# Weight loads in 1 MB pieces at set points, first loads in one queue, and decay ahead of v, q, k

## Chip, cores, metric

One Trainium2 chip, all 8 cores. Each core runs the same program on one prompt sequence and 16 of the 128 sample sequences. The metric is the device time in microseconds (us) of the slowest core. A program on 8 cores has executions in a slower state, in which the cores of one die show a lower granted clock; only fast executions are compared here. In the profiles PE is TensorE (PEld its weight loads), DVE is VectorE, ACT is ScalarE, POOL is GpSimd and SP is SyncE.

## The reference, cut

Two layers of a decoder trunk, for 2,064 prompt tokens per sequence (16 learned meta tokens ahead) and 4 new tokens of every sample sequence:

```python
xn = rmsnorm(h, norm_g)
q, k, v, ga, u, gb, alow, mg = split(xn @ w_in)          # 6160 columns
la = log_sigmoid(alow @ w_alpha + b_alpha) / 16          # data-dependent decay, per key channel
# branch A: gated linear attention with decay exp(cumsum(la)), recurrent state S (128 x 256 per head)
# branch B: trailing means over 2/4/8/16 positions minus the token, a small linear map
ya = (norm(o) * gain * silu(ga)) @ w_a
yb = (pool * scale * silu(gb)) @ w_b
h = h + (sig(mg_A) * ya + sig(mg_B) * yb) @ w_out
```

Outputs are the final normed activations and the new attention and pooling states.

## The kernel before

Each layer has two phases. Phase 1 walks over the prompt in 8 pairs of 128-token tiles (p = 0 to 7) and a last tile of 80 tokens (16 prompt, 64 sample): projections, decay, attention, pooling. Phase 2 walks over the pairs again: `merge` (output gates, `w_a`, `w_b`; 8 column blocks c a pair) and `out_tile` (`w_out`), with the work on the 16 sample states spread between the merges.

The weights of the two phases do not fit together. They share two SBUF regions, V (v, q, k; later six of the merge blocks) and RR (gates, u; later the last two merge blocks and `w_out`). So four times 17 to 19 MB of f32 weights are read and cast to bf16 on the way, which the kernel does on the POOL queue. All other transfers go through the SP queue.

Every operation goes into a list. A small scheduler with modelled durations then fixes the order on each engine ahead of time: lowest list index first among those ready by its model. Each engine executes its order strictly in order, and semaphores are derived from overlaps of memory. So an engine that waits for one thing holds up what is listed behind it.

```python
def load_w1_v(l, after):                 # v, q, k of layer l: 5 pieces
    for a, b in ((0, O_Q), (O_Q, O_K), (O_K, O_V), (O_V, O_V + 4096), (O_V + 4096, N_V1)):
        dma(V1[:, a:b], w1[l, :, a:b], eng="pool", after=after)
def load_w1_r(l): ...                    # gates, u: 4 pieces of 2 MB, into RR
def load_w2_v(l, after): ...             # merge blocks 0..5: 6 pieces, into V
def load_w2_r(l): ...                    # merge blocks 6, 7 and w_out: 4 pieces, into RR

def front(l, p):                         # normed, transposed input of pair p
    if l == 0:
        for i, t in enumerate(tiles_of(p)):
            h = hb[t % 2][0:n, :]        # two tile buffers
            if t >= 2:
                dma(h, hin[r0:r0 + n, :])
            norm_t(0, h, n, t, xn_of(p)[:, :, i * 128:i * 128 + n])   # ACT, POOL, DVE, 8 PE transposes, DVE
        ...
    elif p < NPAIR:
        dma(xnT[p % 2], XN[1][p], ...)   # layer 1: loaded, phase 2 of layer 0 made it

def phase1(l):
    front(l, 0); front(l, 1); decay(l, 0); decay(l, 1)
    for f_ in (q_proj, k_proj):
        f_(0); f_(1)
    for t in range(4):
        v_proj(t // 2, t % 2)
    for p in range(NPAIR):
        if p >= 2:
            q_proj(p); k_proj(p); v_proj(p, 0)
        if p >= 1:
            decay(l, p + 1)
        if p >= 2:
            v_proj(p, 1)
        k_tok(p, k_)                     # 8 PE transposes of k
        scores(p, 0, q_, k_); gate_a(l, p, 0)
        bo0 = attend(p, 0, q_, v_of(2 * p))
        scores(p, 1, q_, k_); gate_a(l, p, 1)
        normalise(bo0, 128, on[0], 0)
        bo1 = attend(p, 1, q_, v_of(2 * p + 1))
        pool_u(l, p)
        normalise(bo1, 128, on[1], 1)
        gate_b(l, p)
        gate_o(on[0], ...)
        if p + 2 <= NPAIR:
            front(l, p + 2)
        pool_y(l, p)
        gate_o(on[1], ...)
        ...
        if p == 2:
            load_w2_v(l, [len(S.ops) - 1])
    # ... last tile, load_w2_r(l), new states out

def phase2(l):
    sample_load(l, 0); sample_load(l, 1)
    for j in range(NPAIR + 1):           # pairs; c = column blocks
        for c in range(8):
            merge(l, j, c)
            if j > 0 and c in (1, 3):
                out_tile(l, j - 1, c // 2)
            # sample work: state s is loaded, cast on ACT, multiplied, updated, stored
        if j == 2 and l + 1 < NL:
            load_w1_v(l + 1, [len(S.ops) - 1])
    ...
```

(Cuts are marked by dots.)

Of the kernel before, what the change touches and what calls it, by code (L numbers as in the profile page):

```python
# [14 lines left out]
NL = 2  # L15
# [14 lines left out]

O_AL, O_Q, O_K, O_V = 0, 128, 128 + 4096, 128 + 8192
N_V1 = 128 + 8192 + 8192
# [18 lines left out]
class Sched:  # L51
# [69 lines left out]
    def list_schedule(self):  # L121
# [15 lines left out]
        for i in range(n):  # L137
            if npred[i] == 0:
                heapq.heappush(pend[ops[i]["eng"]], (0.0, i))
        order = []  # L140
        while len(order) < n:
            best = None
            for e in engs:
                T = free_t[e]
                while pend[e] and pend[e][0][0] <= T:
                    heapq.heappush(avail[e], heapq.heappop(pend[e])[1])
                if avail[e]:
                    st_, idx = T, avail[e][0]
                elif pend[e]:
                    st_, idx = pend[e][0]  # L150
                else:
                    continue
                if best is None or (st_, idx) < (best[0], best[1]):
                    best = (st_, idx, e)
            st_, idx, e = best
            if avail[e] and avail[e][0] == idx:
                heapq.heappop(avail[e])
            else:
                heapq.heappop(pend[e])
            op = ops[idx]  # L160
            if op["dma"]:
                issue = 60.0 if e == "sp" else 900.0
                free_t[e] = st_ + issue
                dma_free[e] = max(st_ + issue, dma_free[e]) + op["cost"]
                done_t[idx] = dma_free[e] + 1800.0
            else:
                free_t[e] = st_ + op["cost"]
                done_t[idx] = st_ + op["cost"] + op["lat"]
            order.append(idx)
            for j, soft in succ[idx]:  # L170
                rt_ = free_t[e] if soft else done_t[idx]
                if ready_t[j] < rt_:
                    ready_t[j] = rt_
                npred[j] -= 1
                if npred[j] == 0:
                    heapq.heappush(pend[ops[j]["eng"]], (ready_t[j], j))
        self.sim_end = max(done_t)
        if __import__("os").environ.get("SIMEND"): print("sim_end", self.sim_end)
        remap = {old: new for new, old in enumerate(order)}
# [176 lines left out]
def build_nc():  # L356
# [34 lines left out]
    with contextlib.ExitStack() as st:  # L391
# [178 lines left out]
        def dma(out, in_, r=(), w=(), eng="sp", after=(), **kw):  # L570
            nb = 1
            for d_ in list(out.shape):
# [4 lines left out]
            return S.add(eng, lambda e: e.dma_start(out=out, in_=in_, **kw), r=list(r) + sb_r, w=list(w) + sb_w,  # L577
                         dma=True, after=after, cost=nb / 220.0)

# [9 lines left out]

        cft = f32(base, NCF)  # L590
        h_first = [dma(hb[t], hin[128 * t:128 * (t + 1), :]) for t in range(2)]
        dma(cft, cf_d[:, :])
        dma(cols, cols_d[:, :])
        cp("dve", ident_f, cft[:, CF_ID:CF_ID + 128])
        cp("dve", ident_b, cft[:, CF_ID:CF_ID + 128])
# [12 lines left out]

        def load_w1_v(l, after):
            for a, b in ((0, O_Q), (O_Q, O_K), (O_K, O_V), (O_V, O_V + 4096), (O_V + 4096, N_V1)):  # L610
                dma(V1[:, a:b], w1[l, :, a:b], eng="pool", after=after)

        def load_w1_r(l):
            for a, b in ((0, 4096), (4096, 8192), (8192, 12288), (12288, N_R1)):
                dma(RR[:, a:b], w1[l, :, N_V1 + a:N_V1 + b], eng="pool")

        def load_w2_v(l, after):
            for c in range(N_EARLY_C):
                dma(V2[:, c * CB:(c + 1) * CB], w2[l, :, c * CB:(c + 1) * CB], eng="pool", after=after)

        def load_w2_r(l):
            o = N_EARLY_C * CB
            a = 0
            for b in (CB, 2 * CB, 2 * CB + 4096, N_R2):
                dma(RR[:, a:b], w2[l, :, o + a:o + b], eng="pool")
                a = b

# [37 lines left out]
        def front(l, p):  # L665

            if l == 0:
                for i, t in enumerate(tiles_of(p)):
                    r0, n = rows(t)
                    h = hb[t % 2][0:n, :]  # L670
                    if t >= 2:
                        dma(h, hin[r0:r0 + n, :])
                    norm_t(0, h, n, t, xn_of(p)[:, :, i * 128:i * 128 + n])
# [8 lines left out]

        WQ, WK, WV = V1[:, O_Q:O_K], V1[:, O_K:O_V], V1[:, O_V:N_V1]
        WGA, WU, WGB, WPW = RR[:, 0:O_U], RR[:, O_U:O_GB], RR[:, O_GB:O_PW], RR[:, O_PW:O_PW + 512]
# [294 lines left out]
        def phase1(l):  # L979
            memset("dve", alow[0:17, :], 1.0)  # L980
            dma(walpha[0:17, :], walpha_d[l])
            front(l, 0)
            front(l, 1)
            decay(l, 0)
            decay(l, 1)
            for f_ in (q_proj, k_proj):
                f_(0)
                f_(1)
            for t in range(4):
                v_proj(t // 2, t % 2)  # L990
            for p in range(NPAIR):
                q_, k_ = qk_of(p)
                if p >= 2:
                    q_proj(p)
                    k_proj(p)
                    v_proj(p, 0)
                if p >= 1:
                    decay(l, p + 1)
                if p >= 2:
                    v_proj(p, 1)  # L1000
                k_tok(p, k_)
                scores(p, 0, q_, k_)
                gate_a(l, p, 0)
                bo0 = attend(p, 0, q_, v_of(2 * p))
                scores(p, 1, q_, k_)
                gate_a(l, p, 1)
                normalise(bo0, 128, on[0], 0)
                bo1 = attend(p, 1, q_, v_of(2 * p + 1))
                pool_u(l, p)
                normalise(bo1, 128, on[1], 1)  # L1010
                gate_b(l, p)
                gate_o(on[0], 128, V(eg, 8, 256)[:, :, 0:128], V(oTg[0], 8, 256)[:, :, 0:128])
# [4 lines left out]
                if p < NPAIR - 1:  # L1017
                    dma(OT[p], oTg[0], w=[("OT", p)])
                if p == 2:
                    load_w2_v(l, [len(S.ops) - 1])  # L1020

# [10 lines left out]
            v_proj(p, 0)  # L1032
            load_w2_r(l)
            k_tok(p, k_)
# [132 lines left out]
        def phase2(l):  # L1167
            if l == NL - 1:
                dma(fg, fg_d[:, :])
            for k in range(3):  # L1170
                load_h(l, k)
            sample_load(l, 0)
            sample_load(l, 1)
            bT = banks.one()
# [6 lines left out]
            done = 0  # L1181
            total = 7 * 8 + 2
            for j in range(NPAIR + 1):
                if j + 1 < NPAIR:
                    p2_loads(l, j + 1)
                for c in range(8):
                    merge(l, j, c)
                    if j > 0 and c in (1, 3):
                        out_tile(l, j - 1, c // 2)
                    k = j * 8 + c + 1  # L1190
                    while done < len(units) and done * total < k * len(units):
# [6 lines left out]
                if j == 2 and l + 1 < NL:  # L1198
                    load_w1_v(l + 1, [len(S.ops) - 1])
            out_tile(l, NPAIR, 0)  # L1200
            if l + 1 < NL:
                load_w1_r(l + 1)

        P2_ORDER = [NPAIR - 1] + list(range(NPAIR - 1)) + [NPAIR]
        P2_TILES = [t for p in P2_ORDER for t in tiles_of(p)]
        load_w1_v(0, [h_first[0]])
        load_w1_r(0)
        for l in range(NL):
# [62 lines left out]
```

## Time and profile before

| | before |
|---|---|
| time, median of 3 | 1431.89 us (1428.2 to 1583.76, the last slow) |
| span of the profiled core | 1427.6 us |
| PE (TensorE matmul) busy | 1226.5 us, 86% |
| k transposes of pair 0, layer 0, start at | 115.75 us |
| PE idle at the two phase boundaries | 21.0 and 17.9 us |
| one pair of phase 1, layer 0 / layer 1 | 41.6 / 40.4 us |

The page gives busy tenths in 40 equal slices of 35.7 us. The first two slices of PE are nearly empty, while DMA is at 90% and more:

```profile
span 1427.6 us, 28242 instructions; the slowest of 8 cores (1415.4 to 1427.6 us)
...
PE   0188889998898599699999988999889859999997
...
DMA  9910115710006654975427210641110765455321
```

The chain of work that ended last, in order of time (start, duration, what), says what the start waits for: a table of 36 KB, then two input tiles, which took 29 and 16 us where the median of such a tile is 4.4 us:

```profile
2.44 21.71 DMA arena<-cols
25.99 29.20 DMA arena<-hin
58.63 16.11 DMA arena<-hin
```

The timeline (start, duration, engine, line, operation, and in brackets the idle time before it and what ended that) shows the other holes in PE. At the first boundary SP can issue the sample-state loads (`sgla`) only at 475.40, ACT casts the first at 480.00, and PE had been idle for 20.98 us. The hole at 598.18 is in phase 2 of layer 0, where five weight loads were issued together at 570.37 just ahead of a sample-state load. The hole at 1156.46 is the second boundary.

```profile
475.40 1.56 SPq L577 DMA_DIRECT2D arena<-sgla  x3
480.00 1.06 ACT L532 ACTIVATE arena<-arena 128x1024 bf16<-128x1024 f32 x1 [21.44 <-DMA arena<-sgla]
481.11 19.21 PE L505 MATMUL psum<-arena 128*128 128x4 bf16 x164 [20.98 <-ACT arena L532]
...
570.37 2.77 POOL L577 DMA_DIRECT2D arena<-w  x5 [1.81 <-DMA nsg_s<-arena]
...
598.18 1.03 PE L511 MATMUL psum<-arena 128*128 128x128 bf16 x8 [11.86 <-DVE arena L552]
...
1156.46 8.77 PE L505 MATMUL psum<-arena 128*128 128x4 bf16 x66 [17.86 <-ACT arena L532]
```

In the table of stretches (stretch, length, busy us of PE, PEld, DVE, ACT and POOL with counts, then granted PE clock, DMA share, GB/s), the first two lines cover the boundaries, the others one steady pair of each layer:

```profile
435.00:500.00 65.00, 42.62 (x389) 34.43 (x389) 17.24 (x41) 16.04 (x31) 17.73 (x35) 0.82 0.75 185
1110.00:1180.00 70.00, 50.13 (x453) 40.06 (x455) 20.81 (x47) 18.83 (x36) 20.70 (x41) 0.85 0.71 185
...
280.50:322.10 41.60, 37.86 (x317) 28.79 (x317) 24.10 (x35) 20.91 (x39) 17.37 (x31) 1.00 0.11 41
...
999.20:1039.60 40.40, 36.79 (x302) 27.92 (x301) 20.58 (x31) 18.83 (x35) 15.91 (x27) 1.00 0.10 33
```

So PE idles for 22 us in the 65 of the first boundary and 20 in the 70 of the second, and for 3.6 to 3.7 us in a pair.

### The profile page before, as it was taken

How to read it: one execution, taken by the hardware profiler on the slowest of the kernel's cores; microseconds unless marked ns; L12 is line 12 of the kernel's file. 1: busy time of each engine (PE TensorE's matmuls, PEld its weight loads, DVE VectorE, ACT ScalarE, POOL GpSimd, SP SyncE). 2: the span in 40 equal slices, each digit the busy share in tenths (PEclk: the TensorE clock that was granted, in tenths of full speed). 3: DMA queues.
4: the chain of work that ended last, by engine and by line, in shares of the span. 5: the costliest groups of instructions: out<-in, count | busy, mean ns of one | idle time of the engine just before them, and what ended most of it. 6: DMA issues, size and time to landing. Idle time of an engine off the chain costs nothing.

```text
span 1427.6 us, 28242 instructions; the slowest of 8 cores (1415.4 to 1427.6 us)
## 1 busy us (share of the span) xinstructions
PE 1226.5 (86%) x10552; PEld 949.4 (67%) x10600; DVE 625.7 (44%) x942; ACT 525.7 (37%) x1020; POOL 476.7 (33%) x812
## 2 busy tenths in 40 slices
PE   0188889998898599699999988999889859999997
PEld 0056667667676477588877666676777648778875
DVE  1133555556454244344435255445554324444433
ACT  1025445444542233133334354444445223323332
POOL 2004534344445132222222253434444513232222
PEclk9979799999999699899999999999999979999999
DMA  9910115710006654975427210641110765455321
GB/s 169 197 49 16 52 68 125 164 48 30 23 24 128 209 186 170 178 246 182 171 84 137 54 47 29 125 106 38 38 38 1 143 209 186 170 176 179 142 89 64
DMA packets 41894, 160.28 MB, mean 112 GB/s; under 512 B 5196, under 2 KB 5324, under 8 KB 39164
## 3 DMA queue, kind: packets, MB, share of 16 engines
q1 hardware_dynamic: 36284, 122.49, 24.8%
q0 software_dynamic: 5472, 35.98, 15.6%
q8 instruction: 83, 1.36, 0.4%
q14 instruction: 55, 0.45, 0.1%
HBM read 139.98 MB, written 55.18 MB: 137 GB/s over the span
## 4 chain that ended last, share of the span: by engine, by line
PE 71%; DMA 11%; DVE 8%; issue 4%; ACT 4%; POOL 2%; SPq 1%; DVEq 0%; POOLq 0%; ACTq 0%
PE psum L505 70%; DVE arena L557 6%; DMA nsp_s<-arena 4%; ACT arena L532 3%; DMA arena<-hin 3%; DMA arena<-sgla 2%; DMA arena<-cols 2%; DVE arena L545 1%; PE psum L511 1%; POOL arena L545 1%; POOL arena L552 1%; SPq L577 0%; POOL arena L577 0%; DVE arena L552 0%; DVEq L252 0%
## 5 line engine op out<-in xcount | busy, mean ns | idle before, releaser
L505 PE MATMUL psum<-arena 128*128 128x256 bf16 (+6 forms) x9840 | 1187.2, 281 | 110.0 <-ACT arena L532 61.4
L505 PEld LDWEIGHTS psum<-arena 128*128 128x128 bf16 (+3 forms) x9888 | 904.7, 101 | 376.5 <-ACT arena L532 81.8
L557 DVE SCALAR_TENSOR_TENSOR arena<-arena,psum 128x256 f32<-128x256 f32 (+4 forms) x454 | 262.6, 608 | 370.6 <-PE psum L505 225.3
L545 POOL TENSOR_TENSOR arena<-arena 128x256 bf16<-128x256 f32 (+13 forms) x321 | 275.4, 861 | 266.7 <-DVE arena L557 223.9
L552 POOL TENSOR_SCALAR arena<-arena 128x256 bf16<-128x256 f32 (+5 forms) x389 | 168.0, 441 | 578.3 <-PE psum L505 259.5
L532 ACT ACTIVATE arena<-psum 128x256 bf16<-128x256 f32 (+9 forms) x308 | 198.5, 658 | 336.6 <-PE psum L505 318.9
L532 ACT ACTIVATE arena<-psum,arena 128x256 f32<-128x256 f32 (+2 forms) x356 | 146.9, 456 | 268.6 <-PE psum L505 215.1
L532 ACT ACTIVATE arena<-arena 128x1024 bf16<-128x1024 f32 (+2 forms) x137 | 138.6, 1027 | 261.8 <-DVE arena L557 125.1
L545 DVE TENSOR_TENSOR arena<-psum,arena 128x1024 bf16<-128x1024 bf16 (+4 forms) x120 | 124.6, 1039 | 182.9 <-PE psum L505 129.1
L557 DVE SCALAR_TENSOR_TENSOR arena<-psum,arena 128x256 bf16<-128x256 f32 (+4 forms) x124 | 90.6, 763 | 80.2 <-PE psum L505 79.4
L511 PE MATMUL psum<-arena 128*128 128x128 bf16 (+3 forms) x712 | 55.0, 226 | 81.5 <-DVE arena L552 67.6
L511 PEld LDWEIGHTS psum<-arena 128*128 128x128 bf16 (+3 forms) x712 | 46.7, 101 | 91.6 <-DVE arena L552 68.8
L557 DVE SCALAR_TENSOR_TENSOR arena<-arena 128x256 bf16<-128x256 f32 (+4 forms) x97 | 67.1, 709 | 7.5 <-POOL arena L545 7.2
L552 DVE TENSOR_SCALAR arena<-arena 128x1024 bf16<-128x1024 f32 (+4 forms) x45 | 29.2, 669 | 62.0 <-POOL arena L545 46.5
L552 DVE TENSOR_SCALAR arena<-psum,arena 128x256 bf16<-128x256 f32 (+1 forms) x68 | 29.7, 478 | 59.7 <-POOL arena L545 48.6
L532 ACT ACT_TABLE_LOAD x32 | 41.1, 1283 | 28.2 <-PE psum L505 21.6
L707 DVE TENSOR_TENSOR_SCAN arena<-arena 128x1024 f32<-128x1024 bf16 (+1 forms) x18 | 38.2, 2121 | 8.1 <-ACT arena L532 8.1
L564 POOL COPY arena<-arena 128x4 f32<-128x4 f32 (+4 forms) x56 | 13.6, 242 | 78.3 <-ACT arena L532 59.4
L577 POOL DMA_DIRECT2D arena<-w x38 | 21.4, 578 | 20.3 <-DMA OT<-arena 10.1
L532 ACT ACTIVATION_READ_ACCUMULATOR arena<-psum 128x1 f32 (+1 forms) x136 | 27.0, 199 | 0.0
L532 ACT ACTIVATION_READ_ACCUMULATOR arena<-arena 128x1 f32 (+1 forms) x51 | 9.6, 188 | 0.0
L564 DVE COPY arena<-arena 128x128 f32<-128x128 f32 (+2 forms) x3 | 0.5, 195 | 12.7 <-DMA arena<-cf 12.7
(8 smaller groups left out, 6.3 us busy)
## 6 DMA issues: line engine op xcount, KB each, us to landing
arena<-w POOLq DMA_DIRECT2D x18, 1024.0 KB, 27.0
arena<-hin SPq DMA_DIRECT2D x32, 512.0 KB, 4.4
arena<-sgla SPq DMA_DIRECT2D x32, 512.0 KB, 5.7
nsg_s<-arena SPq DMA_DIRECT2D x32, 512.0 KB, 3.2
arena<-w POOLq DMA_DIRECT2D x16, 896.0 KB, 19.9
arena<-XN SPq DMA_DIRECT2D x22, 512.0 KB, 4.5
H<-arena SPq DMA_DIRECT2D x16, 512.0 KB, 2.8
arena<-H SPq DMA_DIRECT2D x16, 512.0 KB, 4.2
```

Of the source, the lines that this page charges most:

```text
L505: return S.add("pe", lambda e: e.matmul(out, lhsT=lhsT, rhs=rhs, start=start, stop=stop, skip_group_check=sgc), r=[lhsT, rhs], w=[out], co ...
L511: return S.add("pe", lambda e: e.transpose(out, in_, ident), r=[in_, ident], w=[out], cost=c, lat=250.0, attach=True)
L532: return S.add("act", lambda e: e.activation(out=out, in_=in_, func=func, **kw), r=r, w=w, cost=c)
L545: return S.add(eng, lambda e: e.tensor_tensor(out=out, in0=in0, in1=in1, op=op), r=[in0, in1], w=[out], cost=c)
L552: return S.add(eng, lambda e: e.tensor_scalar(out=out, in0=in0, **kw), r=r, w=[out], cost=ecost(eng, fsz(out), 0.55, [out] + r))
L557: return S.add("dve", lambda e: e.scalar_tensor_tensor(out=out, in0=in0, scalar=scalar, in1=in1, op0=op0, op1=op1), r=r, w=[out], cost=eco ...
L564: return S.add(eng, lambda e: e.tensor_copy(out=out, in_=in_), r=[in_], w=[out], cost=ecost(eng, fsz(out), 0.55, (out, in_)))
L577: return S.add(eng, lambda e: e.dma_start(out=out, in_=in_, **kw), r=list(r) + sb_r, w=list(w) + sb_w, dma=True, after=after, cost=nb / 220.0)
L707: S.add("dve", lambda e: e.tensor_tensor_scan(out=B, data0=rm[:, 0:4 * n], data1=A, initial=0.0, op0=ALU.mult, op1=ALU.add), r=[rm[:, 0:4 ...
```

## The change

Its intent: let no weight burst crowd out the small transfers on which PE waits; read the first weights in the order in which they are needed; and in each pair put the long decay chain (matmul, exponentials, scan) under the v matmuls.

1. Weights move in pieces of about 1 MB. Except at the start, `pace()` issues one piece at a set point of the compute, after the operation listed just before it (and two pieces without that wait at each phase boundary).
2. First layer: one queue, in the order alpha, v, q, k, gates, u. Input tiles 2 and 3 go into that queue too. The constants lead the other queue.
3. The pair loop has a new order, and the start runs v ahead of q and k.
4. Sample work in phase 2 starts one pair of merges later.

The core of the diff (cut; the rest moves the column offsets of v, q, k on both sides, and the scheduler's modelled DMA rate):

```diff
-        h_first = [dma(hb[t], hin[128 * t:128 * (t + 1), :]) for t in range(2)]
         dma(cft, cf_d[:, :])
         dma(cols, cols_d[:, :])
+        for t in range(2):
+            dma(hb[t], hin[128 * t:128 * (t + 1), :])
...
+        W1V = [(0, O_V)] + [(O_V + 2048 * i, O_V + 2048 * (i + 1)) for i in range(8)]
+        W1R = ...; W2V = ...; W2R = ...      # pieces of 1792 to 2560 columns
+        def pace(n_=1, after=True):
+            for _ in range(n_):
+                if queue:
+                    d_, s_ = queue.pop(0)
+                    dma(d_, s_, eng="pool", after=[len(S.ops) - 1] if after else ())
...
-                        dma(h, hin[r0:r0 + n, :])
+                        dma(h, hin[r0:r0 + n, :], eng="pool" if t < 4 else "sp")
...
             front(l, 0)
             front(l, 1)
+            if l == 0:
+                pace(len(queue), False)
...
                 if p >= 2:
+                    decay(l, p)
+                    v_proj(p, 0)
+                    v_proj(p, 1)
                     q_proj(p)
                     k_proj(p)
-                    v_proj(p, 0)
-                if p >= 1:
-                    decay(l, p + 1)
-                if p >= 2:
-                    v_proj(p, 1)
                 k_tok(p, k_)
+                gate_a(l, p, 0)
                 scores(p, 0, q_, k_)
-                gate_a(l, p, 0)
-                bo0 = attend(p, 0, q_, v_of(2 * p))
                 scores(p, 1, q_, k_)
                 gate_a(l, p, 1)
+                bo0 = attend(p, 0, q_, v_of(2 * p))
+                pool_u(l, p)
                 normalise(bo0, 128, on[0], 0)
                 bo1 = attend(p, 1, q_, v_of(2 * p + 1))
-                pool_u(l, p)
+                if p == 2:
+                    plan(V2, w2[l], 0, W2V)
+                pace()
+                gate_b(l, p)
                 normalise(bo1, 128, on[1], 1)
-                gate_b(l, p)
...
-            load_w2_r(l)
+            plan(RR, w2[l], N_V2, W2R)
+            pace(2, False)
...
-            total = 7 * 8 + 2
+            total = 6 * 8 + 2
...
+                    if c % 2 == 0 or j == 0:
+                        pace()
-                    k = j * 8 + c + 1
+                    k = j * 8 + c + 1 - 8
+                    if k == -1:
+                        sample_load(l, 0)
+                        sample_load(l, 1)
...
-                    load_w1_v(l + 1, [len(S.ops) - 1])
+                    plan(V1, w1[l + 1], 0, W1V)
```

More of the change, by code (lines that the diff above doesn't have):

```diff
@@ L28 @@
 WINDOWS = (2, 4, 8, 16)
-O_AL, O_Q, O_K, O_V = 0, 128, 128 + 4096, 128 + 8192
+O_AL, O_V, O_Q, O_K = 0, 128, 128 + 8192, 128 + 8192 + 4096
 N_V1 = 128 + 8192 + 8192
@@ L140, in list_schedule @@
         order = []
+        start_t = {}
         while len(order) < n:
@@ L177, in list_schedule @@
         self.sim_end = max(done_t)
-        if __import__("os").environ.get("SIMEND"): print("sim_end", self.sim_end)
         remap = {old: new for new, old in enumerate(order)}
@@ L577, in dma @@
             return S.add(eng, lambda e: e.dma_start(out=out, in_=in_, **kw), r=list(r) + sb_r, w=list(w) + sb_w,
-                         dma=True, after=after, cost=nb / 220.0)
+                         dma=True, after=after, cost=nb / (310.0 if eng == "pool" else 200.0))
         def bank(bs):
@@ L606, in build_nc, with plan @@
         memset("dve", V(rmm_b, 4, NM)[:, :, NS:NS + 1], 0.0)
-        def load_w1_v(l, after):
-            for a, b in ((0, O_Q), (O_Q, O_K), (O_K, O_V), (O_V, O_V + 4096), (O_V + 4096, N_V1)):
-                dma(V1[:, a:b], w1[l, :, a:b], eng="pool", after=after)
-        def load_w1_r(l):
-            for a, b in ((0, 4096), (4096, 8192), (8192, 12288), (12288, N_R1)):
-                dma(RR[:, a:b], w1[l, :, N_V1 + a:N_V1 + b], eng="pool")
-        def load_w2_v(l, after):
-            for c in range(N_EARLY_C):
-                dma(V2[:, c * CB:(c + 1) * CB], w2[l, :, c * CB:(c + 1) * CB], eng="pool", after=after)
-        def load_w2_r(l):
-            o = N_EARLY_C * CB
-            a = 0
-            for b in (CB, 2 * CB, 2 * CB + 4096, N_R2):
-                dma(RR[:, a:b], w2[l, :, o + a:o + b], eng="pool")
-                a = b
+        W1V = [(0, O_V)] + [(O_V + 2048 * i, O_V + 2048 * (i + 1)) for i in range(8)]
+        W1R = [(2048 * i, 2048 * (i + 1)) for i in range(7)] + [(14336, N_R1)]
+        W2V = [(CB // 2 * i, CB // 2 * (i + 1)) for i in range(2 * N_EARLY_C)]
+        W2R = [(CB // 2 * i, CB // 2 * (i + 1)) for i in range(2 * (8 - N_EARLY_C))]
+        W2R += [((8 - N_EARLY_C) * CB + 2048 * i, (8 - N_EARLY_C) * CB + 2048 * (i + 1)) for i in range(4)]
+        queue = []
+        def plan(dst, src, off, pieces):
+            for a, b in pieces:
+                queue.append((dst[:, a:b], src[:, off + a:off + b]))
+        def pace(n_=1, after=True):
[3 more added lines that the diff above has]
+                    dma(d_, s_, eng="pool", after=[len(S.ops) - 1] if after else ())
         def cblock(c):
@@ L681, in proj @@
                 mm(dst, W[:, kc * wd + c0:kc * wd + c0 + 128], xn[:, kc, 0:n], kc == 0, kc == 7)
-        WQ, WK, WV = V1[:, O_Q:O_K], V1[:, O_K:O_V], V1[:, O_V:N_V1]
+        WQ, WK, WV = V1[:, O_Q:O_K], V1[:, O_K:N_V1], V1[:, O_V:O_Q]
         WGA, WU, WGB, WPW = RR[:, 0:O_U], RR[:, O_U:O_GB], RR[:, O_GB:O_PW], RR[:, O_PW:O_PW + 512]
@@ L983, in phase1 @@
             front(l, 1)
+            if l == 0:
+                pace(len(queue), False)
             decay(l, 0)
             decay(l, 1)
-            for f_ in (q_proj, k_proj):
-                f_(0)
-                f_(1)
             for t in range(4):
                 v_proj(t // 2, t % 2)
+                if l > 0:
+                    pace()
+            for f_ in (q_proj, k_proj):
+                for p in range(2):
+                    f_(p)
+                    if l > 0:
+                        pace()
             for p in range(NPAIR):
@@ L993, in phase1 @@
                 if p >= 2:
+                    decay(l, p)
+                    v_proj(p, 0)
+                    v_proj(p, 1)
                     q_proj(p)
                     k_proj(p)
-                    v_proj(p, 0)
-                if p >= 1:
-                    decay(l, p + 1)
-                if p >= 2:
-                    v_proj(p, 1)
                 k_tok(p, k_)
+                gate_a(l, p, 0)
                 scores(p, 0, q_, k_)
-                gate_a(l, p, 0)
-                bo0 = attend(p, 0, q_, v_of(2 * p))
                 scores(p, 1, q_, k_)
                 gate_a(l, p, 1)
+                bo0 = attend(p, 0, q_, v_of(2 * p))
+                pool_u(l, p)
                 normalise(bo0, 128, on[0], 0)
                 bo1 = attend(p, 1, q_, v_of(2 * p + 1))
-                pool_u(l, p)
+                if p == 2:
+                    plan(V2, w2[l], 0, W2V)
+                pace()
+                gate_b(l, p)
                 normalise(bo1, 128, on[1], 1)
-                gate_b(l, p)
                 gate_o(on[0], 128, V(eg, 8, 256)[:, :, 0:128], V(oTg[0], 8, 256)[:, :, 0:128])
@@ L1018, in phase1 @@
                     dma(OT[p], oTg[0], w=[("OT", p)])
-                if p == 2:
-                    load_w2_v(l, [len(S.ops) - 1])
+                pace()
+            decay(l, NPAIR)
             p = NPAIR
@@ L1171, in phase2 @@
                 load_h(l, k)
-            sample_load(l, 0)
-            sample_load(l, 1)
             bT = banks.one()
@@ L1189, in phase2 @@
                         out_tile(l, j - 1, c // 2)
-                    k = j * 8 + c + 1
+                    if c % 2 == 0 or j == 0:
+                        pace()
+                    k = j * 8 + c + 1 - 8
+                    if k == -1:
+                        sample_load(l, 0)
+                        sample_load(l, 1)
                     while done < len(units) and done * total < k * len(units):
@@ L1198, in phase2 @@
                 if j == 2 and l + 1 < NL:
-                    load_w1_v(l + 1, [len(S.ops) - 1])
+                    plan(V1, w1[l + 1], 0, W1V)
+            if l + 1 < NL:
+                plan(RR, w1[l + 1], N_V1, W1R)
+                pace(2, False)
             out_tile(l, NPAIR, 0)
-            if l + 1 < NL:
-                load_w1_r(l + 1)
         P2_ORDER = [NPAIR - 1] + list(range(NPAIR - 1)) + [NPAIR]
         P2_TILES = [t for p in P2_ORDER for t in tiles_of(p)]
-        load_w1_v(0, [h_first[0]])
-        load_w1_r(0)
+        plan(V1, w1[0], 0, W1V)
+        plan(RR, w1[0], N_V1, W1R)
         for l in range(NL):
@@ L1228 @@
         wv = part(w_in[l])
-        cols_ = [wv[:, :, C_AL:C_AL + 16], wv[:, :, C_Q:C_K], wv[:, :, C_K:C_V], wv[:, :, C_V:C_GA],
+        cols_ = [wv[:, :, C_AL:C_AL + 16], wv[:, :, C_V:C_GA], wv[:, :, C_Q:C_K], wv[:, :, C_K:C_V],
                  wv[:, :, C_GA:C_GA + 512], wv[:, :, C_GA + 512:C_U], wv[:, :, C_U:C_GB], wv[:, :, C_GB:C_AL], pool_w[l].transpose(1, 0, 2)]
```

## The prediction

> **What bounds the kernel now.** The page's first part has PE busy 1226.5 of 1427.6 us (86%); the chain of waits is 71% PE, 11% DMA, 8% DVE. About 200 us of PE idleness can be won; stretches of 20 us and the timeline show where:
> - Start. PE works 11 us of the first 80. DMA share is about 1.0 until 75 us: first-layer weights are read gates first, then v, q, k, and activation tiles, on the other queue, crawl beside them (the chain holds 21.7 us for the column table, then 29.2 and 16.1 us for input tiles, against a median of 4.4 us). Pair 0 reaches its k transposes at 115.8 us.
> - Both phase boundaries. PE idles 21.0 us before 481 and 17.9 us before 1156, released by the cast of the first sample state, whose load waits for output rows to leave an overlapping buffer (27 us under the second weight burst).
> - Layer 0, phase 2: 11.9 us idle before 598; five weight loads issued together at 570 hold a sample-state load for 21.6 us.
> - Pairs of phase 1: 40.4 us each in layer 1, PE busy 36.8; waits on DVE and ACT, 1 to 2 us each.
> - Phase 2 otherwise has PE busy 19.9 of 20.
>
> **What the change does.** No arithmetic changes; weight bytes stay, in twice as many transfers. An issue costs POOL 0.58 us: some 22 us more on an engine that is 33% busy, off the path.
> The Trainium skill ("DMA: Bandwidth & Descriptors", Queues, rings and completion order) says that an engine round-robins between queues packet by packet. The crawling tiles agree. Smaller rows and spread issues should keep activations near idle latency.
>
> Costs, from the trace. The weight queue took 15.6% of the span for 72 MB read: 3.1 us per MB alone.
> 1. Start: constants and tiles 0, 1 first, then alpha, v, q, k (8 MB), one gate piece, tile 2, two pieces, tile 3. Tiles 2 and 3 should land near 40 and 48 us. About 24 us of v, q, k remain then, some at the low clock (0.7) seen after idling. k transposes near 78 us instead of 115.8: minus 38.
> 2. First boundary: sample work starts one pair of merges later (27 us, which covers the loads); output weights may come a few us late. Minus 16 of 21.
> 3. The stall at 598: loads now one per 8 us, 3.1 us each. Minus 10; DMA share there rises towards 1.
> 4. Second boundary: minus 15 of 18.
> 5. Pairs: decay first, 6.9 us of v matmuls over its chain, gate projections between scores and attention. Of 3.6 us idle a pair, 1.4 saved: minus 20 over 14 pairs. The least certain term; the scheduler already filled some of it.
> Sum: about 99 us, nearly all on the critical path.
>
> **Prediction: 1332 us, range 1290 to 1378.** Chances: faster by over 2% 0.95, within 2% 0.04, slower 0.01.
>
> **What would show it.** k transposes of pair 0 at 70 to 85 us; idle at each boundary under 6 us with no sample load as releaser; no PE wait over 4 us in layer 0's phase 2; a pair at 38.5 to 39.5 us; PE busy still about 1220, share 92%.
>
> **What would make it wrong.** Tiles 2 and 3 arrive behind more weights than I count (start gains under 25). Weight issues that wait for a completed operation block POOL, state casts come late, pairs grow. Paced pieces arrive late: new PE waits on weights. Denser sample work in layer 0 saturates DMA. The other way: pairs fall to PE's 36.8 us (30 us more). A lower granted clock once PE idles less would give a few per cent back.

## The result, and the profile after

The changed kernel takes **1359.08 us** (median of 3, 1358.01 to 1359.25), against 1431.89. The ratio of the fast runs is 0.950 (95% interval 0.947 to 0.953). A ratio here is the mean time of one kernel's fast runs over that of the other's of the same rounds, so it is not quite the ratio of the medians.

```profile
span 1357.5 us, 28419 instructions; the slowest of 8 cores (1347.9 to 1357.5 us)
...
PE   3299889988998899989999989999998979999997
...
DMA  9931221432126865889423510222231955665511
```

PE's busy time has not moved (1226.7 us after 1226.5); idle time has gone. Marks in the two timelines say where. The marks are the k transposes of pair 0 and the first merge of each layer:

| stretch | before | after | difference |
|---|---|---|---|
| start to k transposes of pair 0, layer 0 | 115.8 | 100.1 | -15.6 |
| from there to the first merge (phase 1, layer 0) | 329.5 | 329.5 | 0.0 |
| to the k transposes of pair 0, layer 1 (phase 2, layer 0, and the start of layer 1) | 354.5 | 332.7 | -21.8 |
| to the first merge (phase 1, layer 1) | 321.8 | 298.8 | -23.0 |
| to the end (phase 2, layer 1) | 306.1 | 296.4 | -9.7 |

The start is still bound by input tiles. The chain of the changed kernel over its first 110 us:

```profile
2.44 13.18 DMA arena<-hin
...
17.59 30.57 DMA arena<-hin
...
51.46 10.23 DMA arena<-hin
...
68.94 31.36 PE psum L505 x183
```

The first line is tile 1; the column table, 21.71 us before, has left the chain. Tile 2 was issued at 17.59, when tile 0 had freed its buffer, and took 30.57 us. The third line is not tile 3 but tile 4. The DMA view gives tile 3, issued at 20.34 us, 35.9 us to landing, so it was there at 56.2. ACT, however, has the squares of tile 4 ahead of those of tile 3 in its order, and tile 4 could only be issued at 51.46, when tile 2 had left the buffer. So tile 3 waited nearly 7 us for ACT, until 63.0.

The holes at the boundaries are small now, with new entries (`arena<-w`, weights) among the releasers:

```profile
454.38 3.41 PE L505 MATMUL psum<-arena 128*128 128x256 bf16 x36 [2.32 <-ACT arena L532]
460.14 6.06 PE L505 MATMUL psum<-arena 128*128 128x256 bf16 x34 [2.35 <-ACT arena L532]
467.75 7.78 PE L505 MATMUL psum<-arena 128*128 128x512 bf16 x60 [1.55 <-DMA arena<-w]
...
587.53 8.09 PE L505 MATMUL psum<-arena 128*128 128x4 bf16 x55 [5.07 <-ACT arena L532]
...
1100.39 29.86 PE L505 MATMUL psum<-arena 128*128 128x512 bf16 x238 [4.36 <-DMA arena<-w]
```

In stretches again, the boundaries and one pair of each layer:

```profile
420.00:480.00 60.00, 52.23 (x479) 41.89 (x480) 19.98 (x42) 17.75 (x36) 22.67 (x42) 0.97 0.79 184
1045.00:1125.00 80.00, 70.06 (x681) 55.43 (x679) 29.05 (x52) 26.64 (x51) 30.23 (x53) 0.94 0.71 175
...
251.97:296.43 44.46, 39.49 (x318) 29.84 (x317) 24.19 (x35) 21.08 (x39) 18.94 (x33) 0.92 0.24 58
...
934.25:972.75 38.50, 37.02 (x302) 27.97 (x301) 20.65 (x30) 19.15 (x35) 17.43 (x29) 1.00 0.26 59
```

PE idles 7.8 us in the 60 of the first boundary and 9.9 in the 80 of the second. The pairs are the surprise: in layer 1 a pair went from 40.4 to 38.5 us as intended, but in layer 0 it went **up**, from 41.6 to 44.5, and the granted clock in it down to 0.92. The two layers run the same pair loop. The difference is `front`: in layer 0 it norms and transposes two input tiles near the end of the pair, in layer 1 it only loads.

The timeline of a layer-0 pair's end shows it. PE takes 24 transposes in a row (8 of the attention output, 16 of the two normed tiles), waits 2.98 us for DVE (line 557), which is busy with pooling and gate operations, and then 1.89 us more until DVE has emptied the banks of the normed tiles (1.21 us each, the second from 240.36 on):

```profile
233.90 1.50 PE L511 MATMUL psum<-arena 128*128 128x128 bf16 x24
...
235.46 0.28 PE L505 MATMUL psum<-arena 128*128 128x256 bf16 x1
...
238.72 1.01 PE L505 MATMUL psum<-arena 128*128 128x256 bf16 x4 [2.98 <-DVE arena L557]
238.83 1.21 DVE L545 TENSOR_TENSOR arena<-psum,arena 128x1024 bf16<-128x1024 bf16 x1
...
240.36 1.21 DVE L545 TENSOR_TENSOR arena<-psum,arena 128x1024 bf16<-128x1024 bf16 x1
...
241.62 0.61 PE L505 MATMUL psum<-arena 128*128 128x512 bf16 x1 [1.89 <-DVE arena L545]
```

The waits have a second cost. Stretches around them show the granted clock fall to one half, within the first wait (which ends at 238.72) and before PE works again:

```profile
234.00:238.00 4.00, 1.69 (x26) 1.32 (x23) 3.38 (x5) 3.83 (x9) 4.00 (x6) 1.00 0.00 0
238.00:239.00 1.00, 0.28 (x2) 0.25 (x3) 1.00 (x3) 0.00 (x0) 0.95 (x3) 0.52 0.00 0
239.00:244.50 5.50, 3.61 (x19) 1.90 (x18) 4.98 (x9) 0.84 (x2) 4.04 (x10) 0.50 0.85 184
245.00:249.00 4.00, 4.00 (x20) 2.21 (x18) 1.59 (x3) 0.95 (x2) 0.24 (x1) 1.00 0.87 250
```

The Trainium skill ("TensorE: Matmul & The Clock Gate", Why this matters for your kernels) asks for no idle gap over about 3 us between bursts of matmuls, since one idle window puts the array back to half its clock. The trace agrees on the half (0.50). One wait is enough: in all four layer-0 pairs of this kind the clock falls inside the 2.98 us wait, and in the pair shown it comes back only at about 245, after the second wait. But the length of a gap alone does not decide. In the kernel before, a pair's longer wait is 2.0 to 2.1 us, and the clock fell for about 3.4 us after 5 of 12 such waits. Two waits of 2.04 us, which end at 923.31 and at 1005.77, differ:

```profile
918.00:923.50 5.50, 3.46 (x34) 2.90 (x33) 2.98 (x4) 4.19 (x5) 0.85 (x4) 1.00 1.03 160
923.60:926.90 3.30, 3.30 (x17) 2.36 (x16) 2.29 (x6) 2.00 (x9) 3.22 (x8) 0.50 1.00 163
...
1001.00:1006.00 5.00, 2.96 (x30) 2.43 (x29) 2.47 (x4) 3.93 (x4) 0.89 (x4) 1.00 0.00 0
1006.00:1010.00 4.00, 4.00 (x39) 3.60 (x37) 2.36 (x6) 2.52 (x10) 3.83 (x10) 1.00 0.00 0
```

What else decides is not shown here.

### The profile page after: what moved, and what is told of

It reads as the page before. It is cut to its first block, busy times and chain, and to the rows that moved or that the text cites. A ratio compares the mean times of both kernels' runs of the same rounds, so it can differ in the third digit from the quotient of the medians.

```text
span 1357.5 us, 28419 instructions; the slowest of 8 cores (1347.9 to 1357.5 us)
## 1 busy us (share of the span) xinstructions
PE 1226.7 (90%) x10600; PEld 945.8 (70%) x10600; DVE 626.6 (46%) x942; ACT 529.3 (39%) x1020; POOL 501.9 (37%) x850
## 3 DMA queue, kind: packets, MB, share of 16 engines
q0 software_dynamic: 10944, 37.03, 17.8%
## 4 chain that ended last, share of the span: by engine, by line
PE 70%; DMA 10%; POOL 7%; DVE 5%; issue 4%; ACT 2%; SPq 0%; POOLq 0%; DVEq 0%; ACTq 0%
PE psum L505 68%; DVE arena L557 4%; POOL arena L545 4%; DMA arena<-hin 4%; POOL arena L552 3%; PE psum L511 2%; DMA arena<-w 2%; DMA arena<-sgla 2%; ACT arena L532 2%; DMA nsg_s<-arena 1%; DMA nsp_s<-arena 1%; DVE arena L545 0%; DVE arena L706 0%; SPq L577 0%; ACT L532 0%
## 5 line engine op out<-in xcount | busy, mean ns | idle before, releaser
L505 PE MATMUL psum<-arena 128*128 128x256 bf16 (+4 forms) x9888 | 1189.2, 280 | 71.6 <-DVE arena L557 27.0
L505 PEld LDWEIGHTS psum<-arena 128*128 128x128 bf16 (+2 forms) x9888 | 898.9, 100 | 337.7 <-issue 43.0
L545 POOL TENSOR_TENSOR arena<-arena 128x256 bf16<-128x256 f32 (+13 forms) x321 | 280.6, 878 | 246.8 <-DVE arena L557 227.0
L511 PE MATMUL psum<-arena 128*128 128x128 bf16 (+4 forms) x712 | 64.5, 234 | 50.2 <-DVE arena L552 44.0
L511 PEld LDWEIGHTS psum<-arena 128*128 128x128 bf16 (+4 forms) x712 | 51.0, 106 | 64.5 <-DVE arena L552 45.7
L577 POOL DMA_DIRECT2D arena<-w x74 | 43.9, 598 | 88.8 <-DMA OT<-arena 56.7
L532 ACT ACT_TABLE_LOAD x32 | 41.1, 1283 | 25.2 <-PE psum L505 14.4
L564 POOL COPY arena<-arena 128x4 f32<-128x4 f32 (+4 forms) x56 | 12.3, 219 | 92.2 <-ACT arena L532 89.4
## 6 DMA issues: line engine op xcount, KB each, us to landing
arena<-w POOLq DMA_DIRECT2D x38, 512.0 KB, 14.9
```

Source lines behind the costliest of these rows:

```text
L505: return S.add("pe", lambda e: e.matmul(out, lhsT=lhsT, rhs=rhs, start=start, stop=stop, skip_group_check=sgc), r=[lhsT, rhs], w=[out], co ...
L511: return S.add("pe", lambda e: e.transpose(out, in_, ident), r=[in_, ident], w=[out], cost=c, lat=250.0, attach=True)
L532: return S.add("act", lambda e: e.activation(out=out, in_=in_, func=func, **kw), r=r, w=w, cost=c)
L545: return S.add(eng, lambda e: e.tensor_tensor(out=out, in0=in0, in1=in1, op=op), r=[in0, in1], w=[out], cost=c)
L564: return S.add(eng, lambda e: e.tensor_copy(out=out, in_=in_), r=[in_], w=[out], cost=ecost(eng, fsz(out), 0.55, (out, in_)))
L577: return S.add(eng, lambda e: e.dma_start(out=out, in_=in_, **kw), r=list(r) + sb_r, w=list(w) + sb_w, dma=True, after=after, cost=nb / (3 ...
```

## Experiments

Eleven kernels ran in three sessions, each on one chip with the kernel before beside them, 3 rounds each. All gave correct results. The chips differ a little (the kernel before took 1426 us in the session of runs i, j and k, and 1430 in the others), so that differences of a few us between sessions are read from the ratios. The text quoted under each edit is what was expected before the run. k0 below is the start of the k transposes of pair 0 in layer 0; pair lengths are read from one decay scan to the next. The theory for the shortfall against the prediction had two parts: the start loses because tiles 2 and 3 stand in the weight queue, and layer 0's pairs lose because the norm sits at their end. The rivals were that the sheer arrival of the weights binds the start, and that the weight traffic, or a POOL blocked by paced issues, slows the pairs.

### Loads alone: a_loads_only

The changed kernel with the body of the pair loop put back (`decay(l, NPAIR)` after the loop goes too):

```diff
                 if p >= 2:
-                    decay(l, p); v_proj(p, 0); v_proj(p, 1); q_proj(p); k_proj(p)
+                    q_proj(p); k_proj(p); v_proj(p, 0)
+                if p >= 1:
+                    decay(l, p + 1)
+                if p >= 2:
+                    v_proj(p, 1)
                 ...                          # and scores, gates, attention, pooling as before
```

> The changed kernel with the body of the pair loop put back to the old order (q, k, v, then the decay of the next pair, scores before gates); the new loads, the deferred sample work and the new start stay. If the parts simply add, the start keeps its 16 us (k transposes of pair 0 near 100 us), the two phase-2 stretches keep their 22 and 10 us, layer 1's pairs go back from 38.5 to about 40.4 us and layer 0's from 44.5 to about 41.6: about 1380 us, ratio to the kernel before 0.965 to 0.97. Rival: the paced weight issues themselves slow layer 0's pairs; then they stay at 44 us here and the time is near 1395.

1379.97 us, ratio 0.965 (0.963 to 0.968). k0 is at 100.2 us, layer 0's pairs take 41.6, layer 1's 40.4 (two of them 42.1, as in the kernel before). The loads alone are worth about 51 us, and paced issues do not slow the pairs.

### Order alone: b_order_only

The kernel before with the new loop body and nothing else:

```diff
-                if p >= 2:
-                    q_proj(p); k_proj(p); v_proj(p, 0)
-                if p >= 1:
-                    decay(l, p + 1)
-                ...
+                if p >= 2:
+                    decay(l, p); v_proj(p, 0); v_proj(p, 1); q_proj(p); k_proj(p)
+                ...                          # gates ahead of scores and attention, as in the change
```

> The kernel before with only the new body of the pair loop (decay, v, q, k; gates before scores); old loads, old start. Adding up, layer 1's pairs fall to 38.5 us, layer 0's rise to about 44.5, start and boundaries stay: about 1405 us, ratio 0.98 to 0.985. Rival: layer 0's slow pairs come from the loads; then both layers' pairs are near 38.5 to 39 and the time is near 1385.

1403.87 us, ratio 0.982 (0.980 to 0.983). Layer 1's pairs take 38.3 to 39.5 us, layer 0's 44 to 46 while they hold a full norm. So the slow pairs come with the order and not with the loads. The product of the two ratios (0.948) is close to that of the whole change (0.950): the parts nearly add.

### Tiles ahead of the weights: c_tiles_early

```diff
-                    h = hb[t % 2][0:n, :]
+                    h = eg[0:n, (t - 2) * 1024:(t - 1) * 1024] if t in (2, 3) else hb[t % 2][0:n, :]
```

`eg` is the gate buffer, idle until pair 0's gates. With no buffer to wait for, tiles 2 and 3 head the weight queue.

> The changed kernel with one edit: input tiles 2 and 3 go to the gate buffer, which is free at the start, instead of waiting for the two tile buffers, so they are issued ahead of all weights. Theory: the start is bound by tile 2 and 3 landing at 48 and 62 us behind 9 and more MB of weights; then they land before 15 us, PE runs v, q, k as these arrive and pair 0's k transposes come at 58 to 68 us instead of 100: minus 25 to 40 us, ratio to the kernel before about 0.925. Rival: the 17 MB of weights, all in by about 78 us, bound pair 0 in any case; then under 12 us are won.

1330.46 us, ratio 0.930 (0.929 to 0.932), 29 us below the changed kernel. The DMA view of the issues between 1 and 4 us has all four tiles landing in 11 us (last column), and k0 comes at 66.27:

```profile
arena<-hin POOLq DMA_DIRECT2D x2, 512.0 KB, 10.7
arena<-hin SPq DMA_DIRECT2D x2, 512.0 KB, 10.6
```

```profile
66.27 0.61 PE L511 MATMUL psum<-arena 128*128 128x128 bf16 x8
```

(The 62 us for tile 3 in the expectation were tile 4's, misread then; tile 3 landed at 56.2.) The theory holds. The rival has a share that now shows: PE waits 2.65 and 3.71 us for v weights at 31 and 35 us.

### Tiles on the other queue: i_tiles_sp

```diff
-                        dma(h, hin[r0:r0 + n, :], eng="pool" if t < 4 else "sp")
+                        dma(h, hin[r0:r0 + n, :], eng="sp")
```

> The changed kernel with input tiles 2 and 3 issued on the SP queue again, still into the two tile buffers; the weights keep their order. Theory: what makes the tiles late is their place in the weight queue, behind 9 and 11 MB; on the other queue they start at about 18 us and take turns with the weights, so they land near 30 and 40 us instead of 48 and 62, k transposes of pair 0 come at 80 to 90 us instead of 100, and 8 to 18 us are won. Rival: a tile beside the weights is as slow on either queue (21 us a tile in the kernel before); then they land near 40 and 60 us and under 5 us change.

1337.05 us, ratio 0.937 (0.936 to 0.939), 22 us below the changed kernel by the times and 18 by the ratios. k0 is at 74.32. Tiles 2 and 3, issued between 14 and 22 us, took 17.9 us to land in the median, in place of 30.6 and 35.9:

```profile
arena<-hin SPq DMA_DIRECT2D x2, 512.0 KB, 17.9
```

So one part of the change, "all first loads in one queue in order of need", cost about 20 us of what the rest of it won: a tile that can only be issued at 17.6 us gets behind 9 MB of weights that are issued already, whatever its place in the order of need. The edit is to the queue alone: same buffers and the same weight order, and a tile issued at 14.45 in place of 17.59. But the scheduler answered it: ACT now takes tile 3 (at 38.27) ahead of tile 4 (at 47.20), so a part of the 20 us, up to the 7 us above, can be that order. The path from POOL as such is not slower: in run c two tiles from POOL landed in 10.7 us and two from SP in 10.6.

### Larger first pieces: j_big_pieces

```diff
-        plan(V1, w1[0], 0, W1V)
-        plan(RR, w1[0], N_V1, W1R)
+        plan(V1, w1[0], 0, [W1V[0]] + [(W1V[i][0], W1V[i + 1][1]) for i in range(1, 9, 2)])
+        plan(RR, w1[0], N_V1, [(W1R[i][0], W1R[i + 1][1]) for i in range(0, 8, 2)])
```

> The changed kernel with the first layer's weights in pieces twice as large (rows of 16 KB in place of 8 KB), in the same order and queue. Theory: piece size does nothing for the start, order does: k transposes stay at 100 us, time within 4 us of 1359. Rival: smaller rows let the tiles on the other queue through faster; then tile 1 lands well after 15.7 us, and the start is 5 us or more longer.

Two of four executions were slow, so there is no interval; the fast ones took 1363.94 and 1367.46, 5 to 8 us more than the changed kernel by the times, about 11 against the kernel before of the same session. The run is not clean. With larger pieces the scheduler put *all* 17 MB ahead of tiles 2 and 3, which landed about 70 us after the start, with k0 at 106.0. One reading stands by itself: tile 1, on the other queue, was ready for ACT at 19.82 us and not at 15.71. One core is little evidence for this (the eight cores of the changed kernel show 14.4 to 18.5 us), but the medians of the eight cores differ as well, 18.7 us with large pieces and 15.1 with small ones. So wider rows seem to slow the transfers beside them. The Trainium skill ("DMA: Bandwidth & Descriptors", Queues, rings and completion order) says that an engine takes turns between queues by the packet; these 3.6 us agree with that and do not prove it.

### Norm at the head of the pair: d_front_early

```diff
+        xn3 = bf(A_.top, 2048)               # over ktok_m ... qtail, unused until the last tile
         ktok_m = new_bf(512)
...
-            return V(xnT[p % 2], 8, 256) if p < NPAIR else V(xnT_m, 8, NM)
+            return V((xnT + [xn3])[p % 3], 8, 256) if p < NPAIR else V(xnT_m, 8, NM)
...
+                if l == 0 and p + 2 <= NPAIR:
+                    front(l, p + 2)
                 k_tok(p, k_)
...
-                if p + 2 <= NPAIR:
+                if l > 0 and p + 2 <= NPAIR:
                     front(l, p + 2)
```

The third buffer is needed because the pair in work still reads its own input. (The two transfers that write and store it follow suit.)

> The changed kernel with the norm of pair p+2 of layer 0 moved from the end of pair p to its head (after k), for which a third buffer for the normalised input is laid over buffers that are unused until the last tile. Theory: layer 0's pairs take 44.5 us against 38.5 in layer 1 because these norms fall into the crowded end of the pair; they should drop to 39 to 40 us: about 25 us off, ratio to the kernel before about 0.932. Rival: the lower granted clock or the weight traffic slows them; then they stay above 43.

1339.18 us, ratio 0.936 (0.934 to 0.938), 20 us below the changed kernel. A layer-0 pair takes 39.6 us; its stretch:

```profile
237.37:276.98 39.61, 38.06 (x318) 28.85 (x317) 24.31 (x34) 21.20 (x39) 18.90 (x33) 1.00 0.27 66
```

The 4.9 us won per pair are 3.4 us of waiting (44.46 less 39.49 busy, against 39.61 less 38.06) and 1.4 us of PE busy time, with the clock back at 1.00. No weight issue was edited (DMA share 0.27, 0.24 before), so the weight traffic falls as a rival. The lower clock is real, but it came with the waits and went with them: 1.4 of the 4.9 us. The run changes the place of the norm and the number of buffers together; the waits that it removes were for DVE's operations, which speaks for the place.

### What removed the boundary stalls: e_w2r_burst, f_no_defer

Run e issues the last eight pieces of the second weights at once. Run f spreads the sample work from the first merge on, as before.

```diff
 # e_w2r_burst
             plan(RR, w2[l], N_V2, W2R)
-            pace(2, False)
+            pace(8, False)
 # f_no_defer
+            sample_load(l, 0)
+            sample_load(l, 1)
...
-            total = 6 * 8 + 2
+            total = 7 * 8 + 2
-                    k = j * 8 + c + 1 - 8
+                    k = j * 8 + c + 1        # and no loads at k == -1
```

> The changed kernel with the eight last pieces of the second weights issued all at once at the phase boundary, where the change issues two and then one per merge. Theory: pacing delays the output weights, whose waits the changed kernel shows (7.9 us in all); then these waits go and 4 to 8 us are won. Rival: the DMA engines are full there either way (share 1.0), so only the order shifts and the time stays at 1359 plus or minus 4 us, with longer waits on sample states.

> The changed kernel with the sample work spread from the first merge on as before (two state loads issued ahead of it); pacing stays. Theory: the boundary stalls went because the sample work was deferred by one pair of merges; then PE idles 15 to 20 us again at each boundary behind the first state's cast, and the time rises by 15 to 30 us to about 1380. Rival: the paced weight pieces alone removed them; then the time stays within 6 us of 1359.

Run e: 1358.16 us, ratio 0.949 (0.942 to 0.956), the same as the changed kernel. The weight waits went; at the first boundary one of 5.11 us for ACT, behind a state load, and one of 3.12 us for POOL came in their place (5.92 and 2.98 at the second). Its rival was right: the order shifted. Run f: 1365.97 us, ratio 0.953 (0.948 to 0.959), 7 us more (8 more than run e of the same session), where I had expected 15 to 30; at each boundary one wait is back at half its old size:

```profile
454.89 4.29 PE L505 MATMUL psum<-arena 128*128 128x4 bf16 x30 [10.85 <-ACT arena L532]
...
1094.02 8.39 PE L505 MATMUL psum<-arena 128*128 128x4 bf16 x63 [10.60 <-ACT arena L532]
```

PE's longest single wait for ACT, which casts the sample states, at the first and the second boundary, all with the new pair order (the fourth corner is run b):

| | sample work at once | sample work deferred |
|---|---|---|
| second weights in a burst | 14.9, 12.3 us (b) | 5.1, 5.9 us (e) |
| second weights paced | 10.9, 10.6 us (f) | 2.4, 1.6 us (changed kernel) |

(Run b bursts all the second weights, in the larger pieces of the kernel before; run e only the last eight.) Deferring the sample work does most of it, pacing some. With the old pair order the same corner as the changed kernel (run a) still waits 11.6 and 9.0 us, so the static order on ACT has its part too. I have not taken that apart.

### Layer 1's first weights in a burst: g_w1v_burst

```diff
                 if j == 2 and l + 1 < NL:
                     plan(V1, w1[l + 1], 0, W1V)
+                    a_ = len(S.ops) - 1
+                    while queue:
+                        d_, s_ = queue.pop(0)
+                        dma(d_, s_, eng="pool", after=[a_])
```

> The changed kernel with the nine first pieces of layer 1's weights issued in one go after the third pair of merges, as before, in place of one per two merges. Theory: a burst holds a sample-state load for some 20 us; PE's wait there grows from 5 us to about 12, so 5 to 8 us are lost (about 1366). Rival: the wait in layer 0's second phase comes from the denser sample work; then nothing changes.

1370.73 us, ratio 0.957 (0.952 to 0.962): 12 us are lost, more than I had expected. The stall is back, larger than the 11.86 us of the kernel before:

```profile
556.72 0.37 PE L505 MATMUL psum<-arena 128*128 128x4 bf16 x8 [13.80 <-ACT arena L532]
```

Of the two bursts tried, this one cost 12 us and run e's nothing.

### Both cures: h_tiles_front, and with moved buffers: k_best

Run h has the edits of c and d. Run k also lays the three sample-state buffers, which overlap outputs still on their way out at the boundary, over memory that comes free earlier:

```diff
         A_.top = mid
+        S_in = [new_f32(1024) for _ in range(3)]
+        hb.append(new_f32(1024))
         oTg.append(new_bf(2048))
...
-        hb.append(new_f32(1024))
-        S_in = [new_f32(1024) for _ in range(3)]
```

> The changed kernel with both cures together: tiles 2 and 3 loaded ahead of the weights, and the norm of pair p+2 moved to the head of pair p with a third buffer. They act in different stretches, so they should add: 28 and 20 us off 1359, about 1311 us, ratio to the kernel before 0.915 to 0.92. If the weights' arrival (78 us) now binds pair 0 to 2, up to 8 us less is won.

> Both cures of the run before (1304 us), and the three sample-state buffers laid over memory that comes free before the last outputs of the first phase leave. Theory: what is left of PE's wait at each boundary (2 to 5 us on the cast of a state) is the state load waiting for those output rows; then it goes, 3 to 8 us are won, about 1298 us, ratio to the kernel before 0.905 to 0.91. Rival: the DMA engines are full there (share 1.0) and only the order shifts; then 1304 plus or minus 3 us, with more waits on weights.

Run h: **1303.88 us**, ratio 0.910 (0.905 to 0.915), k0 at 70.4, layer-0 pairs 39.6. It beats both kernels; c won 29 us and d 20, together 55, which is their sum within run h's interval (about 7 us to each side). Run k: 1304.19 us, ratio 0.914 (0.913 to 0.916), the same time. Its rival was right. At the first boundary the first state now costs PE a wait of 1.77 us at 376.28, in place of 2.45 us in run h at 402.85, but PE waits more often for weights (1.05, 3.61 and 2.85 us at 399, 412 and 415). The DMA share there is 1.01 to 1.04 from 380 to 410 us: with the engines full, moving one transfer forward moved another back.

## Why the prediction was right or wrong

The time (1359) lies in the range of 1290 to 1378, and the direction was right. The sum was not: 99 us foretold, 73 measured. A range of 88 us left room for that. Of the signs under "What would show it", only a layer-1 pair (38.5 us) and PE's busy time (1226.7 us) came out as named; k0 (100.1 us), the idle time at the boundaries (7.8 and 9.9 us, state casts still among the releasers), the longest wait in layer 0's phase 2 (5.07 us) and a layer-0 pair (44.5 us) did not.

- **Start, minus 38 foretold, minus 15.6 measured.** This step failed, by size: "Tiles 2 and 3 should land near 40 and 48 us ... k transposes near 78 us". They landed at 48.2 and 56.2, tile 3 was used at 63.0, and the PE work left after it took longer than the 24 us named: the 22 us missing are about 8, 7 and 7. The tiles' position in the queue had been counted right. The queue's speed had not: I took 3.1 us per MB, the weight queue's time alone over the whole run, and added a guess for the rest. The 10.0 MB up to and with tile 2 took from 1.5 to 48.2 us, 4.7 us per MB: the queue's own time was 3.4 us per MB read in this stretch, and the other queue held 21% of the DMA engines. Part of the gap stays open: by 48.2 us the queue had landed 5.67 MB as written, 0.4 MB more than tile 2's place in it, so the transfer was not finished when its turn was; uneven engines could do that, but the profile shows no single engine. Then ACT's fixed order added 7 us, which I had not looked for. Last, PE worked without a gap for 31.4 us from 68.94 to k0, the first 12 of them at a clock of 0.50 after the idling. Runs c and i show that the tiles bound the start, and i that their place in the weight queue, with what the scheduler made of it, was the cost. Which part of the new start won the 15.6 us (constants first, v first, the order of the weights) was not taken apart.
- **First boundary and the stall at 598, minus 26 foretold, minus 21.8 measured** over phase 2 of layer 0 and the start of layer 1. Right in mechanism (runs f and g) and nearly in size. One wait of 5.07 us behind a state load is left; whether the denser sample work causes it is not shown.
- **Second boundary, minus 15 foretold, minus 9.7 measured.** "Paced pieces arrive late: new PE waits on weights" was listed as a danger, and it happened: 4.36 us at 1100. Run e shows that issuing them earlier does not help.
- **Pairs, minus 20 over 14 pairs.** The sum is near (the order alone is worth 26 us, run b), the story was half wrong. A layer-1 pair won 1.9 us, where I had said 1.4. Layer 0's pairs 2 to 5 lost 3.1, 3.0, 2.9 and 0.8 us (from the k transposes of one pair to those of the next). Its first two pairs won 7.1 us, though they carry a norm too (why is not shown), and its end 2.6, so that its phase 1 came out at 0.0 in the table. "Gate projections between scores and attention" was costed for both layers alike; I had not asked what layer 0's pairs carry in addition. Run d shows it: the norm at the end of the pair.
- **Clock.** I had feared a lower granted clock once PE idles less. With the change it hardly moved (die medians 0.960 before, 0.961 and 0.962 after). In run h, where PE idles least, it went the other way: 0.985, with PE's busy time down from 1226.7 to 1215.0 us for the same work.
- **POOL.** The 22 us of extra issues cost nothing that shows, as foretold: layer 1's pairs with paced issues take 38.5 us, and 40.4 in run a with the old order, as in the kernel before.

## What to carry to other kernels

"In order of need" held for this queue only as far as its entries could be issued at once: a small transfer that must wait for a buffer belongs ahead of the bulk, in memory that is idle then, or on another queue. Cost a queue's rate from the stretch in question, with its company, not from the whole run. And when one loop body serves two cases (here with and without a norm), look at one trip of each before and after: one got 1.9 us better, the other up to 3.1 us worse, and a sum over the kernel hides it.

## What the Trainium skill lacked or had wrong

- "DMA: Bandwidth & Descriptors" (Issuing engines are not separate DMA queues) says that issuing from several engines "will only save the time on the sequencer it takes to initiate the DMA". Here the same two tiles, issued from SP in place of POOL, took 17.9 us to land (median) in place of 30.6 and 35.9, and the kernel became about 20 us faster, part of which may be ACT's new order: the queues share the engines, but not the line of waiting transfers. The page's section on queues, named above, fits the run better than this sentence.
- The same page (Rules for kernel authors) advises 1 MiB and more per DMA. Halving the pieces (from about 2 MB to 1 MB as read, 1 to 0.5 MB as written) cost little bandwidth: the weight queue took 15.6% of 1427.6 us for 72 MB before, 3.1 us per MB read, and 17.8% of 1357.5 us for 73 MB (with two tiles) after, 3.3. The rule does not weigh the transfers beside a burst: a sample state waited behind one until PE had idled 13.8 us (run g).
- "TensorE: Matmul & The Clock Gate" gives a limit of about 3 us for one gap. Here the clock fell to 0.50 for about 3.4 us after 5 of 12 waits of 2.0 to 2.1 us in the pairs of the kernel before, and inside each of four waits of 2.98 us after the change: a gap below the limit is not safe. The page's section on cycling through PSUM banks says that frequent short idles can make the clock swing, without a number; these waits come once in some 40 us.
